# Batch normalization with ReLU: two-part rows moved to the second half of x, and three matmuls in place of one to spread the parameters

## The chip, the cores and the metric

The kernel runs on one core of one Trainium2 chip. Times are device microseconds of that core. A time quoted for a kernel is the median of its runs; a ratio is the mean time of one kernel's fast runs over that of the other's fast runs of the same rounds, so it isn't quite the ratio of the medians.

## The reference

```python
x = np.random.randn(32, 128, 32, 32)          # float32, 16.78 MB
normalized = (x - running_mean[None, :, None, None]) / np.sqrt(running_var[None, :, None, None] + eps)
scaled = normalized * gamma[None, :, None, None] + beta[None, :, None, None]
return np.maximum(scaled, 0)
```

Per channel this is relu(x * scale + bias), with scale = gamma / sqrt(var + eps) and bias = beta - mean * scale. 16.78 MB are read and as many written.

## The kernel before

The (batch, channel) rows of 1024 numbers are laid out so that each of 128 partitions holds 16 neighbouring channels (J = 16), in two halves of x. All loads of x go out on SyncE's queue, the four parameter loads and all stores on ScalarE's. One matmul with a matrix of zeros and ones copies the 8 x 16 numbers of each parameter to all 128 partitions; a short chain on ScalarE and VectorE makes scale and bias; ScalarE then does one activation for each row and issues a store after each tile.

```python
TILES = ((0, 0, 2), (0, 2, 4), (0, 4, 8), (0, 8, 16), (1, 0, 16))   # half, first row, end
LOAD_CUTS = {(1, 8)}          # the second half is loaded in two pieces of 8 rows
STORE_CUTS = {(0, 1)}         # the first tile is stored row by row
HALVES = {(0, 0), (0, 1)}     # rows that are computed in two activations of 512
...
for c, d in zip(cuts, cuts[1:]):
    nc.sync.dma_start(out=xt[:, c - a : d - a, :], in_=xr[t, :, c:d, :])
...
for k, src in enumerate((running_var, gamma, running_mean, beta)):
    nc.scalar.dma_start(out=raw[:, k, :], in_=src.rearrange("(q j) -> q j", j=J))
...
cols = psum.tile([P, 4, J], F32, name="cols")
nc.tensor.matmul(cols..., rep..., raw..., start=True, stop=True)      # all four parameters
nc.scalar.activation(out=std_t, in_=cols[:, 0, :], func=ACTF.Sqrt, bias=eps_t[:, 0:1], scale=1.0)
nc.vector.reciprocal(out=rstd_t, in_=std_t)
nc.vector.tensor_mul(out=scale_t, in0=cols[:, 1, :], in1=rstd_t)
nc.vector.tensor_mul(out=ms_t, in0=cols[:, 2, :], in1=scale_t)
nc.vector.tensor_sub(out=bias_t, in0=cols[:, 3, :], in1=ms_t)
for t, a, b, xt in tiles:
    for j in range(a, b):
        ...                                             # Relu of row j, in place, whole or in two
        if j + 1 == b or (t, j + 1) in STORE_CUTS:
            nc.scalar.dma_start(out=outr[t, :, first : j + 1, :], in_=xt[...])
```

## Time and profile before

| What | Before |
|---|---|
| Time, median of the first 3 runs | 83.6 us |
| Span in the profile | 82.0 us |
| First row begins, first store goes out | 9.61, 11.16 us |
| Last load of x is there (row begins) | 46.87 us |
| Last store goes out, lands | 56.05, 81.15 us |
| ScalarE busy | 48% of the span |

How to read it: a store goes out when ScalarE issues it, but its bytes move only when the sixteen DMA engines come to them. The distance between going out and landing (25 us for the last store) says how much work stood in the queue, the store's own 8 MB included. The lines themselves are in the prediction.

### The profile page before, as it was taken

To read this page: it belongs to the slowest core of one execution; us is meant where nothing else is said; L and a number is where in the kernel's file an instruction comes from. 1 tells how busy PE (TensorE), PEld (TensorE's weight loads), DVE (VectorE), ACT (ScalarE), POOL (GpSimd) and SP (SyncE) were. 2 spreads that over 40 slices of the span, in tenths; PEclk is the share of its full clock that TensorE was granted. 3 is DMA by queue.
4 is the path that set the end of the run, shared out by engine and by line. 5 is a ranking of instruction groups with operands and counts; after the bars stand their busy time and mean duration, and the time that the engine had idled before them with its cause. 6 is when DMAs were issued, how large, how long until landed. Compare 5 with 4: busy or idle time off the path is not lost.

```text
span 82.0 us, 120 instructions
## 1 busy us (share of the span) xinstructions
PE 0.7 (1%) x2; PEld 0.5 (1%) x2; DVE 0.8 (1%) x5; ACT 39.1 (48%) x36; POOL 0.8 (1%) x6
## 2 busy tenths in 40 slices
PE   0002000000000000000000000000000000000000
PEld 0002000000000000000000000000000000000000
DVE  0000300000000000000000000000000000000000
ACT  0600477799239999199994199993000000000000
POOL 3000000000000000000000000000000000000000
DMA  2899997979899989999799799998992999996590
GB/s 48 336 424 456 416 544 336 524 322 526 338 434 430 506 358 506 390 434 444 320 460 500 316 424 448 512 432 368 480 736 128 416 512 512 512 512 288 224 512 0
DMA packets 1792, 33.56 MB, mean 409 GB/s; under 512 B 256, under 2 KB 256, under 8 KB 512
## 3 DMA queue, kind: packets, MB, share of 16 engines
q1 hardware_dynamic: 864, 16.78, 48.7%
q10 hardware_dynamic: 928, 16.78, 47.6%
HBM read 16.78 MB, written 16.78 MB: 409 GB/s over the span
## 4 chain that ended last, share of the span: by engine, by line
DMA 56%; ACT 10%; issue 2%; SPq 0%
DMA x<-in_x_dram 56%; ACT x L102 10%; SPq L56 0%
## 5 line engine op out<-in xcount | busy, mean ns | idle before, releaser
L102 ACT ACTIVATE x<-x,bias_t,scale_t 128x1024 f32<-128x1024 f32 (+1 forms) x34 | 37.5, 1177 | 9.9 <-DMA x<-in_x_dram 7.6
L86 ACT ACT_TABLE_LOAD x1 | 1.3, 1283 | 2.6 <-issue 2.6
L86 ACT ACTIVATE std_t<-cols,eps_t 128x16 f32<-128x16 f32 x1 | 0.3, 273 | 4.5 <-PE cols L78 4.5
L78 PE MATMUL cols<-raw,rep 8*128 8x64 f32 x2 | 0.7, 429 | 7.6 <-DMA raw<-in_beta_dram 7.6
L78 PEld LDWEIGHTS cols<-raw,rep 8*128 8x128 f32 x2 | 0.5, 306 | 7.6 <-issue 7.6
L68 POOL TENSOR_SCALAR_AFFINE_SELECT rep<-rep 8x128 f32<-8x128 f32 x1 | 0.4, 392 | 0.1
L88 DVE RECIPROCAL rstd_t<-std_t 128x16 f32<-128x16 f32 x1 | 0.3, 254 | 7.7 <-ACT std_t L86 7.7
L67 POOL MEMSET rep<- 8x128 f32 x1 | 0.2, 194 | 0.3 <-POOLq L130 0.3
L90 DVE TENSOR_TENSOR scale_t<-cols,rstd_t 128x16 f32<-128x16 f32 x1 | 0.2, 175 | 0.1
L92 DVE TENSOR_TENSOR ms_t<-cols,scale_t 128x16 f32<-128x16 f32 x1 | 0.2, 175 | 0.0
L94 DVE TENSOR_TENSOR bias_t<-cols,ms_t 128x16 f32<-128x16 f32 x1 | 0.2, 174 | 0.0
L130 POOL MEMSET const-bfloat16-1.0<- 128x1 bf16 x1 | 0.1, 106 | 0.0
L130 POOL MEMSET const-uint8-127<- 128x1 uint8 x1 | 0.1, 106 | 0.0
L130 POOL MEMSET const-float32-0.0<- 128x1 f32 x1 | 0.1, 103 | 0.3 <-issue 0.3
L130 POOL MEMSET const-float32-1.0<- 128x1 f32 x1 | 0.1, 103 | 0.0
L65 DVE MEMSET eps_t<- 128x1 f32 x1 | 0.1, 59 | 0.9 <-PEq L130 0.9
## 6 DMA issues: line engine op xcount, KB each, us to landing
x<-in_x_dram SPq DMA_DIRECT2D x3, 4096.0 KB, 38.7
out_dram<-x ACTq DMA_DIRECT2D x1, 4096.0 KB, 28.7
x<-in_x_dram SPq DMA_DIRECT2D x2, 1024.0 KB, 5.8
x<-in_x_dram SPq DMA_DIRECT2D x1, 2048.0 KB, 11.3
out_dram<-x ACTq DMA_DIRECT2D x1, 2048.0 KB
out_dram<-x ACTq DMA_DIRECT2D x2, 512.0 KB, 19.6
out_dram<-x ACTq DMA_DIRECT2D x1, 1024.0 KB
raw<-in_running_var_dram ACTq DMA_DIRECT2D x1, 0.5 KB
```

The costliest lines, as they stand in the source:

```text
L65: nc.vector.memset(eps_t, float(eps))
L67: nc.gpsimd.memset(rep, 1.0)
L68: nc.gpsimd.affine_select(out=rep, in_=rep, compare_op=mybir.AluOpType.is_equal, fill=0.0, base=0, pattern=[[0, P // Q], [-1, Q]], channel ...
L78: nc.tensor.matmul(cols.rearrange("p k j -> p (k j)"), rep.rearrange("q r s -> q (r s)"), raw.rearrange("q k j -> q (k j)"), start=True, s ...
L86: nc.scalar.activation(out=std_t, in_=cols[:, 0, :], func=ACTF.Sqrt, bias=eps_t[:, 0:1], scale=1.0)
L88: nc.vector.reciprocal(out=rstd_t, in_=std_t)
L90: nc.vector.tensor_mul(out=scale_t, in0=cols[:, 1, :], in1=rstd_t)
L92: nc.vector.tensor_mul(out=ms_t, in0=cols[:, 2, :], in1=scale_t)
L94: nc.vector.tensor_sub(out=bias_t, in0=cols[:, 3, :], in1=ms_t)
L102: nc.scalar.activation(out=xt[:, j - a, w : w + step], in_=xt[:, j - a, w : w + step], func=ACTF.Relu, bias=bias_t[:, j : j + 1], scale=sc ...
L130: nc = _bacc.Bacc("TRN2", target_bir_lowering=False, num_devices=1)
```

## The change

The intent, as far as the code tells it: the square root, the reciprocal and the scale need only variances and gammas, so a first matmul for these two could let them start before means and betas arrive; and whole rows in the first tile bring the first store forward, while the two-part rows go where ScalarE waits anyway.

```diff
-HALVES = {(0, 0), (0, 1)}
+HALVES = {(1, 0), (1, 1)}
 ...
     cols = psum.tile([P, 4, J], F32, name="cols")
-    nc.tensor.matmul(
-        cols.rearrange("p k j -> p (k j)"),
-        rep.rearrange("q r s -> q (r s)"),
-        raw.rearrange("q k j -> q (k j)"),
-        start=True,
-        stop=True,
-    )
+    for a, b in ((0, 2), (2, 3), (3, 4)):
+        nc.tensor.matmul(
+            cols[:, a:b, :].rearrange("p k j -> p (k j)"),
+            rep.rearrange("q r s -> q (r s)"),
+            raw[:, a:b, :].rearrange("q k j -> q (k j)"),
+            start=True,
+            stop=True,
+        )
```

## The prediction

> **What bounds the kernel now.** I first read the page: the span, the share of each engine, the forty slices, the chain that ended last.
>
> ```profile
> span 82.0 us, 120 instructions
> ...
> PE 0.7 (1%) x2; PEld 0.5 (1%) x2; DVE 0.8 (1%) x5; ACT 39.1 (48%) x36; POOL 0.8 (1%) x6
> ...
> ACT  0600477799239999199994199993000000000000
> POOL 3000000000000000000000000000000000000000
> DMA  2899997979899989999799799998992999996590
> ...
> HBM read 16.78 MB, written 16.78 MB: 409 GB/s over the span
> ```
>
> ScalarE, the busiest compute engine, works 48% of the span and is finished in slice 28 of 40. The DMA row stands near 9 from slice 2 to the end; single low digits beside high ones (such as the 2 near 62 us) come from a transfer being booked when its packet ends, so I average over longer stretches. The bound is bytes: 33.56 MB through the DMA engines.
>
> Next, the DMA share and rate in stretches cut at the events of the timeline (the columns are: stretch in us, its length, busy time and instructions of PE, PEld, DVE, ACT, POOL, the clock, the DMA share, GB/s):
>
> ```profile
> 0.00:3.00 3.00, 0.00 (x0) 0.00 (x0) 0.06 (x1) 0.43 (x1) 0.80 (x6) 1.00 0.40 101
> ...
> 3.00:11.16 8.16, 0.66 (x2) 0.50 (x2) 0.78 (x4) 2.64 (x4) 0.00 (x0) 1.00 1.04 441
> 11.16:46.85 35.69, 0.00 (x0) 0.00 (x0) 0.00 (x0) 26.83 (x24) 0.00 (x0) 1.00 1.00 425
> 46.85:81.20 34.35, 0.00 (x0) 0.00 (x0) 0.00 (x0) 9.16 (x8) 0.00 (x0) 1.00 0.98 422
> ```
>
> From 3 us on the share is 1.0, whether only loads run (441 GB/s), loads with stores (425), or stores alone (422, with the tail in it). The engines never starve. The last check is whether a store is always waiting after the loads end. The DMA issues say that the 4 MB store, the last but one, issued at 33.10, lands after 28.7 us, so at 61.8. The last store, 8 MB, is issued at 56.05 and lands 25.1 us later, at 81.15. At 56.05 the queue therefore still holds 61.8 - 56.05 = 5.7 us of older stores. **The start of the last store has 5.7 us of slack; only bytes, and the first 3 us in which little moves, set the end.**
>
> The change touches the parameter stage. Its timeline:
>
> ```profile
> 7.59 0.50 PEld L78 LDWEIGHTS cols<-raw,rep 8*128 8x128 f32 x2 [7.59 <-issue]
> 7.62 0.66 PE L78 MATMUL cols<-raw,rep 8*128 8x64 f32 x2 [7.62 <-DMA raw<-in_beta_dram]
> 8.12 0.33 SPq L56 DMA_DIRECT2D x<-in_x_dram  x1
> 8.31 0.27 ACT L86 ACTIVATE std_t<-cols,eps_t 128x16 f32<-128x16 f32 x1 [4.46 <-PE cols L78]
> 8.62 0.25 DVE L88 RECIPROCAL rstd_t<-std_t 128x16 f32<-128x16 f32 x1 [7.68 <-ACT std_t L86]
> 8.98 0.17 DVE L90 TENSOR_TENSOR scale_t<-cols,rstd_t 128x16 f32<-128x16 f32 x1
> 9.19 0.17 DVE L92 TENSOR_TENSOR ms_t<-cols,scale_t 128x16 f32<-128x16 f32 x1
> 9.40 0.17 DVE L94 TENSOR_TENSOR bias_t<-cols,ms_t 128x16 f32<-128x16 f32 x1
> 9.61 1.52 ACT L102 ACTIVATE x<-x,bias_t,scale_t 128x512 f32<-128x512 f32 x2 [1.02 <-DVE bias_t L94]
> 11.16 0.37 ACTq L110 DMA_DIRECT2D out_dram<-x  x1
> ```
>
> The reader is to see a serial chain of 2.0 us, from the landing of the betas (7.62) to the first row (9.61), and then 1.55 us to the first store. All of it lies in the stretch in which the DMA engines are already full of loads.
>
> **What the Trainium skill says.** (1) "DMA: Bandwidth & Descriptors", section "Queues, rings and completion order": each DMA engine takes turns between the queues that have work, a whole packet at a time. The trace agrees: loads have rows of 8 to 32 KiB, the first stores rows of 4, 4 and 8 KiB, one packet a row, 8 rows for each of 16 engines. From 11.16 on the three 4 MB loads hold 24 packets for each engine; 24 store packets beside them are 8 x (4 + 4 + 8) KiB x 16 = 2.10 MB, and the DMA view of 11.2 to 46.9 us has 2.33 MB on the store queue. (2) Same page, "Where 436 GB/s comes from": the ports' ceiling is 435 GB/s, and for transfers to and from HBM about 358 is said to bind. The trace's 441 and 425 agree with the first and not with the second. (3) "ScalarE: Activation LUTs", "What ACT_TABLE_LOAD costs": an ACTIVATE takes 186 ns + 0.833 ns for each element, 93 ns more for each pointer operand, and neighbours overlap by 93 ns. For two pointers: 1225 ns for 1024 and 799 for 512; the trace has 1227 and 805. (4) "PSUM — Partial Sum Buffer", "PSUM bank collisions raise a hardware error": one engine may not write a bank while another reads it in the same partitions, so waits are to be set by bank. The tile cols is 4 x 16 x 4 = 256 B a partition of a bank of 2 KiB, so all three results share it. The built program agrees: the square root waits for TensorE's count of **three**, all matmuls, and so does the scale's multiply.
>
> **The change, part by part.**
>
> Three matmuls for one. Intended: variances and gammas go ahead while means and betas are in flight, so that square root, reciprocal and two multiplies (8.31 to 9.36) leave the path. That doesn't happen: the square root waits for the third matmul, which waits for the betas. The means are there by 6.87 (the sync engine's wait for them, 4.1 us, ends then), the betas at 7.6. So the first two matmuls run in 0.7 us of idle time, and what follows 7.62 is two passes over 16 columns in place of 64. From 7.62 to 8.28 the passes took 0.66 us. I don't know what share of it goes with the columns; the whole of 0.66 scaled down by 64/16 is an upper bound, 0.5 us, but with pass durations of 416 and 442 ns and 0.50 us of weight loads that don't shrink I take 0.1 us (estimate). If the first two were delayed they would queue: 4 passes of 0.33 us, so up to +0.6 us in place of -0.1. Path to the first row: 9.61 - 0.1 = about 9.5 us.
>
> Halves leave the first tile. A row as a pair takes 1.52 us, whole 1.23: 0.29 us less for each of two rows. The first store goes out at 9.5 + 1.25 = 10.75 (was 11.16, 0.4 earlier), the second and all up to the fifth tile's start 0.7 earlier.
>
> Halves come to the second half of x. Two rows cost 0.29 more each, 0.6 us of ScalarE. They lie in its first eight rows, begun at 34.85 and done at 44.0; ScalarE then idled 2.86 us for the last load (46.87). Hidden, down to some 2.3 us idle.
>
> What the earlier store does: 0.4 us at 26.7 KiB/us for each engine (437 GB/s over 16) is 11 KiB, at most one row of the 16 KiB load. So one more load packet is paired with a store packet, and by the loads' end one more store packet, now of 16 KiB, went between: 16 / 26.7 = 0.6 us later for the last load. ScalarE ends and the last store is issued at up to 56.7 in place of 56.05, still 5 us before the store queue runs dry.
>
> Sum on the path that sets the end: bytes unchanged, the first 3 us unchanged, the tail unchanged: 0. Moving 0.4 us x 441 GB/s = 0.18 MB of loads from the pure stretch to the mixed one at 425 costs 0.18/0.425 - 0.18/0.441 = 0.02 us.
>
> **The rivals.** (a) *The start is worth its time:* if an earlier first store ended the kernel earlier, -0.4 to -0.7 us (0.8%), 82.9 to 83.2. For it: the chain is serial. Against: the DMA share is 1.0 before the store comes. (b) *The bank wait isn't there or the split works as intended:* first row at about 8.5, a store 1.4 us earlier. By the same argument the last load moves by 1.4 us and the end by less than 0.1. (c) *ScalarE or the last load becomes the bound:* later loads plus 0.6 us of halves push the last store beyond 61.8. It takes 5.7 us; I count 0.6. Were the halves' 0.6 us to hit the path it would be 84.2. (d) *Another mix of packets changes the rate or the tail:* 425 against 441 GB/s shows that mixing costs up to 4%; one packet's shift of 0.6 us of that is 0.02 us, but a different end of the 16 engines' last rows (64 KiB, 2.4 us for each) could move the tail by a few tenths either way.
>
> **Range and chances.** The sum is 0, so 83.6 us. The three times before lie within 0.1%. (a) and (d) give -0.5 and +0.5: range 83.1 to 84.1. For over 2% it takes 1.7 us; nothing that I found is that large without the 5.7 us being used up: faster 0.02, same 0.96, slower 0.02.
>
> **What would show it.** Right: six passes on TensorE, the last two begun at the betas' landing; the square root still released by the third, at 8.1 to 8.3; first row near 9.5, first store near 10.75; DMA share 1.0 from 3 us on; last load at 46.9 to 47.5; last store issued at 56 to 57, landed near 81. Wrong: the square root before the betas land; a gap in the DMA row between the older stores and the last one; a landing of the last store moved by more than 0.5 us.

## The result, and the profile after

83.5 us (83.44 to 83.61, 6 runs) against 83.56 (83.48 to 83.71, 6 runs) of the kernel before on the same chip. The ratio is 0.9992, with a 95% interval from 0.9979 to 1.0005: the same, as it lies within 2%.

The page of the changed kernel, lines that answer to those of before:

```profile
span 81.7 us, 128 instructions
...
PE 1.7 (2%) x6; PEld 1.5 (2%) x6; DVE 0.8 (1%) x5; ACT 39.1 (48%) x36; POOL 0.8 (1%) x6
...
ACT  0600477799039999199997199993000000000000
...
DMA  2899999989899898969789699996991999998290
```

TensorE has six passes for two, and the DMA row is as full as it was. The three stretches of before, cut at the same places, with DMA share and GB/s in the last two columns:

```profile
3.00:11.16 8.16, 1.75 (x6) 1.49 (x6) 0.78 (x4) 2.48 (x4) 0.00 (x0) 1.00 1.03 438
11.16:46.85 35.69, 0.00 (x0) 0.00 (x0) 0.00 (x0) 27.18 (x26) 0.00 (x0) 1.00 1.00 429
46.85:81.20 34.35, 0.00 (x0) 0.00 (x0) 0.00 (x0) 9.07 (x8) 0.00 (x0) 1.00 0.97 420
```

The timeline of the changed kernel at the places that moved (start, length, engine and line, what ended the wait before it):

```profile
6.33 1.78 PE L81 MATMUL cols<-raw,rep 8*128 8x32 f32 x6 [6.33 <-DMA raw<-in_gamma_dram]
8.15 0.28 ACT L89 ACTIVATE std_t<-cols,eps_t 128x16 f32<-128x16 f32 x1 [4.21 <-PE cols L81]
...
9.44 1.24 ACT L105 ACTIVATE x<-x,bias_t,scale_t 128x1024 f32<-128x1024 f32 x1 [1.02 <-DVE bias_t L97]
10.71 0.38 ACTq L113 DMA_DIRECT2D out_dram<-x  x1
...
34.78 9.71 ACT L105 ACTIVATE x<-x,bias_t,scale_t 128x512 f32<-128x512 f32 x10 [1.79 <-DMA x<-in_x_dram]
46.77 9.16 ACT L105 ACTIVATE x<-x,bias_t,scale_t 128x1024 f32<-128x1024 f32 x8 [2.27 <-DMA x<-in_x_dram]
55.95 0.34 ACTq L113 DMA_DIRECT2D out_dram<-x  x1
```

The first matmul begins at 6.33, when the gammas are there, 1.3 us earlier than the one matmul of before. But the square root begins at 8.15, after all six passes, and not after the first two. The first row is 0.17 us earlier (9.44 for 9.61) and the first store 0.45 us earlier (10.71 for 11.16). At 46.77, the arrival of the last load, 0.10 us of this is left. The DMA view of 14.5 to 15.0 us shows where the first packets of the first store run, in both kernels. Before, then after (queue, packets, MB, share of 16 engines; a packet is counted where it starts, so a share can pass 100%; q10 is the queue of the stores):

```profile
q10 hardware_dynamic: 7, 0.03, 13.9%
```

```profile
q10 hardware_dynamic: 16, 0.07, 31.8%
```

No store packet runs before 14.5 us in either. The loads now stand in rows of 32 KiB, each of which keeps an engine busy for 1.2 us, and the store packets start in groups between them, in the packet records of the changed kernel from 14.56 to 14.96 us, from 15.94 to 16.32 and so on. Before, 7 packets started in the first group and the others a round later; in the changed kernel all 16 did, one for each engine. So going out 0.45 us earlier moved nine engines' packets one round forward and none before 14.5 us. Counted up to the start of the last load packet, there are 343 store packets before (7 x 22 + 9 x 21) and 352 after (16 x 22). The nine packets more are of 8 KiB, at 0.31 us each; but the 24 load packets of 32 KiB of an engine took 29.29 us in place of 29.58, so the last load came no later.

### The profile page after: what moved, and what is told of

Read it like the earlier page. It is cut to its first block, busy times and chain, and to the rows that moved or that the text cites. A ratio compares the mean times of both kernels' runs of the same rounds, so it can differ in the third digit from the quotient of the medians.

```text
span 81.7 us, 128 instructions
## 1 busy us (share of the span) xinstructions
PE 1.7 (2%) x6; PEld 1.5 (2%) x6; DVE 0.8 (1%) x5; ACT 39.1 (48%) x36; POOL 0.8 (1%) x6
## 4 chain that ended last, share of the span: by engine, by line
DMA 56%; ACT 10%; issue 2%; SPq 0%
DMA x<-in_x_dram 56%; ACT x L105 10%; SPq L56 0%
## 5 line engine op out<-in xcount | busy, mean ns | idle before, releaser
L81 PE MATMUL cols<-raw,rep 8*128 8x16 f32 (+1 forms) x6 | 1.7, 384 | 6.4 <-DMA raw<-in_gamma_dram 6.3
L81 PEld LDWEIGHTS cols<-raw,rep 8*128 8x128 f32 x6 | 1.5, 307 | 6.5 <-issue 6.3
```

Of the source, the lines that this page charges most:

```text
L81: nc.tensor.matmul(cols[:, a:b, :].rearrange("p k j -> p (k j)"), rep.rearrange("q r s -> q (r s)"), raw[:, a:b, :].rearrange("q k j -> q ...
```

## The experiments

Twelve kernels ran; the kernel before ran beside each. All but one start from the changed kernel. The kernel before spread from 83.46 to 84.08 us, more widely than at first; the changed kernel stayed within 83.44 to 83.61 in all twelve of its timed runs.

**One part alone.** First the halves without the split matmul, then the split matmul without the halves:

```diff
 # the kernel before, and only:
-HALVES = {(0, 0), (0, 1)}
+HALVES = {(1, 0), (1, 1)}
```

> One matmul kept, halves moved. Bytes theory: 83.4 to 83.6 us, first row at 9.6 us, first store out at 10.9 (0.3 before the kernel before). Rival, that an earlier first store ends the kernel earlier by the same time: 83.2 to 83.3.

```diff
 # the changed kernel, and only:
-HALVES = {(1, 0), (1, 1)}
+HALVES = {(0, 0), (0, 1)}
```

> Three matmuls, halves left in the first tile. Bytes theory: 83.4 to 83.6 us; the square root still released by the third matmul at about 8.15 us, first row at 9.4 to 9.5, first store at 11.0.

83.54 us with the halves alone (first row at 9.71, first store at 10.98), 83.76 with the matmuls alone (first row at 9.54, first store at 11.08). The kernel before lay between 83.47 and 83.96 in this call, so one look tells neither from it. The first store's packets again begin in the round at 14.5 us, on 15 of 16 engines with the halves moved, on 9 with them in place. From the first row to the first store it is 1.27 us with the halves moved and 1.54 with them in place: the halves, more than the matmuls, carry what there is of an earlier start.

**A bank for each matmul.** Is it the shared PSUM bank that makes the square root wait?

```diff
-    cols = psum.tile([P, 4, J], F32, name="cols")
+    banks = [psum.tile([P, 512], F32, name=f"cols{i}") for i in range(3)]
 # matmul i writes banks[i]; the readers take banks[0] (variances, gammas), banks[1] (means), banks[2] (betas)
```

> The changed kernel with each matmul's result in a bank of its own, so that the square root waits for the first matmul alone. Bank theory: square root at about 7.0 us (8.15 in the changed kernel), first row at about 8.5 (9.44), first store at about 9.8 (10.71). Bytes theory: all the same 83.4 to 83.6 us. Rival (start on the path): 0.9 us less, 82.6. If the first row stays at 9.4, it was not the bank that made the square root wait.

Its timeline:

```profile
5.92 0.60 PE L81 MATMUL cols<-raw,rep 8*128 8x32 f32 x2 [5.92 <-DMA raw<-in_gamma_dram]
6.55 0.27 ACT L89 ACTIVATE std_t<-cols,eps_t 128x16 f32<-128x16 f32 x1 [2.65 <-PE cols L81]
...
8.49 1.24 ACT L105 ACTIVATE x<-x,bias_t,scale_t 128x1024 f32<-128x1024 f32 x1 [1.66 <-DVE bias_t L97]
...
47.90 9.16 ACT L105 ACTIVATE x<-x,bias_t,scale_t 128x1024 f32<-128x1024 f32 x8 [3.18 <-DMA x<-in_x_dram]
```

Now the square root follows the first matmul by 0.03 us, at 6.55, and the first row begins at 8.49: 0.95 us earlier than in the changed kernel. This is what the split was meant to do, so the shared place of the results, one tile in one PSUM bank, is shown to be what prevented it. That it is the bank and not the tile is not shown: the edit gives each matmul both of its own. A variant that was only built, not run, speaks against the bank: with one tile over three banks and one matmul in each, the built program still lets the square root wait for TensorE's count of three, and with three tiles for a count of one. And the kernel isn't faster: 84.11 us, ratio to the kernel before 1.0034 (1.0013 to 1.0055). The rival, that an earlier start ends the kernel earlier, expected 82.6 and is out. That it should be slower, I had not expected. This time the store did catch an earlier round: 7 of its packets stand between 13.0 and 13.5 us, and the last load came 1.13 us later. By the packet records up to the start of the last load packet, about one store packet more of 8 KiB went between on each engine, 0.3 us, and the 24 load packets themselves took 29.94 us in place of 29.29, 0.65 more.

**Parameters ahead of x.** A much earlier start of compute, paid with a later start of the bytes:

```diff
+    for k, src in enumerate((running_var, gamma, running_mean, beta)):
+        nc.sync.dma_start(out=raw[:, k, :], in_=...)
     # loads of x follow on the same queue
-    for k, src in enumerate(...): nc.scalar.dma_start(out=raw[:, k, :], in_=...)
```

> The changed kernel with the four parameter loads issued ahead of the loads of x, on the same queue. Four issues of 0.3 to 0.6 us put the first load of x some 1.3 to 1.6 us later; the parameters land some 4 us earlier, so the first row is at 7 to 8 us (9.44), bound by x's own landing. Bytes theory: later start of the byte stream, 84.8 to 85.2 us. Rival (start of compute on the path): 1.5 to 2 us faster, about 81.8.

```profile
2.23 7.37 SPq L59 DMA_DIRECT2D x<-in_x_dram  x6
...
6.88 1.24 ACT L105 ACTIVATE x<-x,bias_t,scale_t 128x1024 f32<-128x1024 f32 x1 [2.52 <-DMA x<-in_x_dram]
```

The loads of x begin to go out at 2.23 us in place of 0.81; the first row begins at 6.88 in place of 9.44. The time is 85.53 us, ratio 1.0209 (1.0185 to 1.0232): more time, though the interval leaves open whether by more than 2%. So 2.6 us gained at the start of compute did not make up for 1.4 us lost at the start of the byte stream; together they cost about 2 us over the changed kernel's 83.5. Both theories' numbers missed. The direction is that of the bytes; the excess over 1.4 us is taken up below.

**The slack of the last store.**

```diff
+                if (t, j + 1) == (1, J):          # ahead of the last store
+                    for _ in range(8):
+                        nc.scalar.activation(out=pad_t, in_=pad_t, func=ACTF.Relu, ...)   # scratch tile
```

> The changed kernel with eight further activations on a scratch tile ahead of the last store, 8 x 1.15 = 9.2 us: the last store goes out at 65.1 us in place of 55.95, past the 61.6 at which the older stores land. Slack theory (5.6 us): slower by 9.2 - 5.6 = 3.6 us or more, up to 5.5 with the restart of an empty queue: 87.0 to 89.0 us. If the slack is smaller than thought: up to 92.7.

The last store goes out at 64.82 us, and by the view of the DMA issues it lands 20.7 us later:

```profile
64.82 0.34 ACTq L120 DMA_DIRECT2D out_dram<-x  x1
...
out_dram<-x ACTq DMA_DIRECT2D x1, 20.7
```

88.09 us, ratio 1.0512 (1.0488 to 1.0537), as the slack theory had it. It also gives the true slack. A last store that finds the queue empty takes 20.7 us; in the changed kernel it takes 24.9. So it waits 24.9 - 20.7 = 4.2 us behind older stores, not 5.7. The timed runs agree with the profiles: the store went out 64.82 - 55.95 = 8.9 us later, less 4.2 is 4.7, and 88.09 - 83.5 = 4.6 were measured.

**Fewer bytes.**

```diff
+                    if (t, a) != (0, 2):          # no store of the second tile, 1.05 MB
                         nc.scalar.dma_start(out=outr[...], in_=xt[...])
```

> The changed kernel without the store of the second tile, 1.05 MB of 33.56 (its rows of the output are wrong on purpose). Bytes theory: 1.05 MB / 0.437 = 2.4 us less, 81.1 us. If ScalarE or the chain of loads set the end: 83.5.

82.08 us, ratio 0.9789 (0.9763 to 0.9816): less time, though the interval leaves open whether by more than 2%, but by 1.4 us under the changed kernel's 83.5 and not by 2.4. The timeline and the DMA issues say where the rest went:

```profile
49.34 9.16 ACT L105 ACTIVATE x<-x,bias_t,scale_t 128x1024 f32<-128x1024 f32 x8 [4.77 <-DMA x<-in_x_dram]
58.53 0.34 ACTq L115 DMA_DIRECT2D out_dram<-x  x1
...
out_dram<-x ACTq DMA_DIRECT2D x1, 20.7
```

With the store of 8 KiB rows gone, the next store's rows of 16 KiB alternate with the last load instead. The packet records have six of them on each engine before the last load packet starts, where the changed kernel has six of 8 KiB: 48 KiB more, 6.21 us of store packets in place of 4.40. The load packets of 32 KiB took 29.82 us in place of 29.29 besides. That makes 1.8 + 0.5 = 2.3 us; the last load came at 49.34, 2.6 us after 46.77. The last store then goes out at 58.53 and takes 20.7 us, as the store behind the scratch activations did. The slack is gone and ScalarE's path is the bound, the third rival of the prediction. The sum is right to 0.2 us: 58.53 + 20.7 = 79.2 against 55.95 + 24.9 = 80.85, 1.6 us less.

**No alternation at all.** All stores behind the loads on one queue; then the same with the first load on the other queue, to fill the first 3 us.

```diff
-                    nc.scalar.dma_start(
+                    nc.sync.dma_start(             # the stores
```

> The changed kernel with all stores issued from the queue of the loads, so that they stand behind the loads and the two never alternate. If alternating costs rate (441 GB/s in loads alone, 425 to 429 in the mixed 35.7 us): last load lands at 41 to 42 us (46.77), and 35.7 x (1 - 427/440) = 1.0 us less in all, 82.5 us. If only bytes count: 83.4 to 83.6.

```diff
 # the same, and:
+            eng = nc.scalar if (t, c) == (0, 0) else nc.sync
+            eng.dma_start(out=xt[:, c - a : d - a, :], in_=xr[t, :, c:d, :])
```

> The same, and the first load of x goes out on ScalarE's queue ahead of the parameters, beside the second on the other. If the slow first 3 us (88 to 101 GB/s) come from one queue issuing alone: the stream is full some 0.5 us earlier, 0.5 us less than the kernel with the stores behind. Parameters land later, first row at 9 to 11 us: without effect on the end. If the first 3 us are latency: the same time.

84.8 us, ratio 1.0119 (1.0096 to 1.0142), and 84.5 us, ratio 1.0084 (1.0066 to 1.0103). Both expectations missed for the first: the last load is there at 43.36, and the kernel is slower. Stretches of the kernel with the stores behind:

```profile
11.16:40.00 28.84, 0.00 (x0) 0.00 (x0) 0.00 (x0) 23.90 (x24) 0.00 (x0) 1.00 1.03 427
...
40.00:42.00 2.00, 0.00 (x0) 0.00 (x0) 0.00 (x0) 1.97 (x2) 0.00 (x0) 1.00 0.78 262
42.00:44.00 2.00, 0.00 (x0) 0.00 (x0) 0.00 (x0) 0.64 (x1) 0.00 (x0) 1.00 0.69 281
```

Loads alone run at 427 GB/s here, no faster than loads and stores in turns (429). And at the end of the loads, 4 us run at 262 to 281: against 430 that is a loss of about 4 x (1 - 271/430) = 1.5 us. The packet records put it at 1.3: the last two of the 24 packets of 32 KiB took 2211 and 1557 ns on average, where 1213 is usual, and 1216 and 1245 in the changed kernel. 1.3 us is also what the kernel is slower by. So alternating costs no rate, and in it the loads' end ran at nearly full speed. For the second kernel the first row began only at 14.95 us, not at 9 to 11, and the first 3 us moved 90 GB/s against 120, so two queues didn't fill them; its 0.3 us under its twin are again in the load packets (30.26 us for the 24, against 30.60), for a reason that isn't known.

**Earlier and later starts side by side.** Is the own banks' 0.3% real, and does it go on the other way? The changed kernel again, own banks again, and the changed kernel with three or six activations on a scratch tile ahead of the first row:

```diff
+        for _ in range(3):                        # or 6
+            nc.scalar.activation(out=pad_t, in_=pad_t, func=ACTF.Relu, ...)
         for t, a, b, xt in tiles:
```

> The changed kernel itself, to stand beside the next three on the same chip: within 0.15% of the kernel before.

> The kernel with own banks again. If its 0.3% was the chip's doing: within 0.15% of the changed kernel. If an earlier first store costs time, as it seemed: 0.25 to 0.45% over the changed kernel of the same call, last load of x at 47.9 us (46.8).

> The changed kernel with three activations on a scratch tile ahead of the first row (3 x 1.27 = 3.8 us): first store out at 14.5 us (10.7), its packets some three rounds of 1.2 us later. Bytes theory: 83.5 us, as the late start is 3.8 us of ScalarE's idle time before the fourth tile. If the start of compute is on the path: 87.3. If each round in which stores alternate with loads costs about 0.3 us, as the kernel with own banks suggests: 82.6 to 82.9.

> The same with six (7.6 us): first row at 17 us, first store at 18.3, the last store out at 56.5 to 57.5, within its slack of 4.3 us. Bytes theory: 83.5. Start on the path: 91.1. Cost of alternation: 81.7 to 82.3.

The "round" is the mean of sixteen packets of 32 KiB, the load packets sorted by start from the packet records of the trace; "24 rounds" is their sum, what an engine spends on these packets.

| Kernel | Store goes out | Time | Ratio to before | 24 rounds | Last round |
|---|---|---|---|---|---|
| own banks again | 9.32 us | 84.05 us | 1.0035 (1.0007 to 1.0063) | 29.88 us | 1410 ns |
| changed, again | 10.86 us | 83.53 us | 0.9968 (0.9939 to 0.9998) | 29.45 us | 1233 ns |
| three ahead | 14.66 us | 84.36 us | 1.007 (1.0042 to 1.0099) | 30.02 us | 1515 ns |
| six ahead | 18.47 us | 84.5 us | 1.0088 (1.0059 to 1.0116) | 30.12 us | 1667 ns |

Neither "start on the path" (87.3 and 91.1 us for the late ones) nor my "each round of alternation costs 0.3 us" (82.6 and 81.7) holds: delays of 3.8 and 7.6 us cost 0.8 and 1.0 us, and a start 1.5 us earlier costs 0.5. The bytes theory's 83.5 missed as well, by about 1%: bytes and the start of their stream set the time to within 1 us, not to a tenth. The two checks missed too: the changed kernel lay 0.32% under the kernel before, which spread most, and own banks 0.62% over the changed kernel, not 0.25 to 0.45. What differs is in the page's line on the loads' queue (packets, MB, share). The changed kernel again, then six ahead:

```profile
q1 hardware_dynamic: 864, 16.78, 48.5%
```

```profile
q1 hardware_dynamic: 864, 16.78, 48.8%
```

48.5% of 81.8 us is 39.7 us for each engine, 48.8% of 82.7 is 40.4, for the same packets. The stores' packets take 39.0 us in all of them. In the packet records a store packet of one size takes nearly the same time in all runs (1213 ns for 32 KiB, 2418 to 2464 for 64), and a load packet of 32 KiB takes 1213 at best, in rounds with stores beside it too. It takes longer in single rounds: around the one where the stores set in, in the changed kernel most in the seventh (1344 ns), in own banks again also in the 16th to 18th (1289 to 1363), and in the late ones most in the last. The "24 rounds" column accounts for 0.43 of own banks' 0.52 us over the changed kernel, for 0.57 of 0.83 and for 0.67 of 0.97 with three and six ahead. In the kernel with the parameters first, the eight packets of 16 KiB of the third tile took 664 ns in place of 611, 0.4 us in all, which is most of its excess. This is an account of where the time went, not of why. Stores that run beside the last loads are not needed for it: with the stores behind, the first store packet starts at 42.48 us, when the slowest round of loads (2211 ns) is over and all packets of the last have begun. Why a given start is good or bad stays open.

No experiment with a right result beats both kernels.

## Why the prediction was right

**Time.** 83.6 with 83.1 to 84.1; measured 83.5. Right, and for the reason given: the DMA engines are full before the first store comes, and neither bytes nor their start changed. With the parameters first, the bytes started 1.4 us later and compute 2.6 us earlier, and the time rose by 2 us. That the change came out at 0 and not some tenths off was in part luck: own banks and the two late starts move as many bytes from the same start and lie 0.5 to 1.0 us above it.

**The bank wait.** The wait was right: the square root waited for the third matmul and was at 8.15; with own banks it followed the first. That the bank is the reason is not shown, as the three results also shared a tile. The gain of 0.1 us on the path was 0.17 in one profile and 0.07 and 0.02 in others (first row at 9.54 and 9.59). In the first profile the first two matmuls did not lie in idle time: the gammas came at 6.33, and the six passes ran one after the other, 1.78 us. The line merges the six, so it doesn't show the last two begin at the betas' landing.

**The halves.** Right: first store at 10.71 (10.75 forecast), the pair of rows 0.55 us longer in the second half (0.6), hidden in a wait that shrank from 2.86 to 2.27 us (2.3).

**"16 / 26.7 = 0.6 us later for the last load".** Wrong: it came 0.10 us earlier. The step took one packet more of 16 KiB to go between. It was one of 8 KiB (0.31 us), as no packet of 16 KiB of this kernel starts before the last load packet has ended, and only on nine engines of sixteen; and the step took the load packets' time as fixed, where it fell by 0.29 us. The store's bytes also don't move as soon as it goes out, but 3.4 to 4.0 us later beside queued loads (0.85 us in the empty queue of the slack experiment). That packets take turns held: 22 store packets for each engine before the last load packet. The sizes of the shifts need the load packets too: 0.3 + 0.65 us of the 1.13 with own banks, 1.8 + 0.5 of the 2.6 with one store left out.

**"5.7 us of slack".** Too large: 25.1 - 20.7 = 4.4 (4.2 in the changed kernel). A store into an empty queue needs 20.7 us, though its packets take 8 x 2.418 = 19.3; the step left out the 1.4 us of start and landing.

**"Mixing costs up to 4%", and 0.02 us for it.** The reading was wrong: the rows' own DMA shares are 1.04 and 1.00, and 441/1.04 = 424 stands against 425/1.00 = 425, so the two rates differ by what is booked in the stretch. (A transfer is booked where its packet starts, not where it ends, as the prediction has it.) Most rounds with stores beside them are as fast as rounds without, and the kernel without alternation was 1.2% slower. The loss sits in single rounds, around the setting in of the stores and at the end of the loads. The prediction's "few tenths either way" from how the packets fall together was about the right size: own banks show 0.5 us, the late starts up to 1.0, all of it one way.

## What to carry to other kernels

Before shortening a chain at the start, look whether the DMA engines are already full at that time; if they are, an earlier first store only trades places with loads, and the last store's slack is what to measure. To split a matmul so that readers may begin early, give each part a PSUM tile of its own (here each lay in a bank of its own), and check in the built program which count the reader waits for. In a stream of large packets a start moved by 1 to 7.6 us here still moved the end by 0.6 to 1.2%, later each time, so judge such changes with the kernels side by side on one chip. And when two rates of a profile are compared, divide each by its own DMA share first.

## What the Trainium skill lacked or had wrong

- "DMA: Bandwidth & Descriptors", "Where 436 GB/s comes from": that the HBM side binds at about 358 GB/s for transfers to and from HBM is not what this case shows. A packet of 32 KiB takes 1213 ns on each of 16 engines, 432 GB/s, for loads and stores alike, with one core at work. The same page keeps the figure, under its measured table, for two cores of a pair at once, so it is this sentence that lacks the condition.
- The same page, "Queues, rings and completion order": taking turns packet by packet agrees (22 store packets for each engine between the last 23 load packets). It lacks how long a store waits to be let in beside queued loads: 3.4 to 4.0 us from going out to the first packet here.
- The same page has no figure for one queue passing from loads to stores: 262 to 281 GB/s over 4 us, with the last two load packets of an engine at 2211 and 1557 ns.
- No page says that load packets take longer in single rounds, at the end of a load stream among them: up to 1667 ns for 1213 in the last round beside stores, while store packets of 64 KiB stay within 2418 to 2464 ns.
- "PSUM — Partial Sum Buffer", "PSUM bank collisions raise a hardware error": the runs don't separate waiting by bank from waiting by tile. It lacks a figure for what sharing costs: the first row at 9.44 us against 8.49 with a tile and a bank for each matmul.
